# Storing units two by two as 32 KB runs from three output tiles, in a mixture-of-softmaxes kernel bound by its transfers

## The chip, the cores and the metric

One core of one Trainium2 chip. The metric is the device time of one execution in microseconds (us). Executions of the kernel before lie between 780.81 and 781.27 us. All runs told here were of the fast state (none over 1.5% above the fastest of its kernel); where a "slow run" is spoken of in experiment 9, it is the upper of two groups within that state.

## The reference

```python
def reference(logits, prior):            # logits 32x128x4x4096, prior 32x128x4, float32
    prior_probs = softmax(prior)         # over the 4 heads
    softmax = np.exp(logits - logits.max(-1, keepdims=True))
    softmax /= softmax.sum(-1, keepdims=True)          # over the vocabulary of 4096
    return np.sum(prior_probs[..., None] * softmax, axis=2)     # 32x128x4096
```

Cut to what matters: per row, four softmaxes of 4096 numbers are averaged with four weights. 268.5 MB are read and 67.1 MB are written.

## The kernel before

The 4096 rows are cut into 32 units of 128 rows, one row to a partition. Row pairs of a partition lie side by side in memory; a unit takes one row of each pair (`j` is 0 or 1). A unit is loaded into one of two input buffers (64 KB per partition), ACT makes four exponentials with their sums, DVE weights them into an output tile, and ACT's queue stores that tile (16 KB per partition).

```python
ltile = cpool.tile([P, 2, H, V], FP32, name="ltile")      # two input buffers
ebuf1, ebuf3: SBUF tiles; ebuf2: PSUM tile                # exponentials 1, 3, 2
obuf = cpool.tile([P, 2, V], FP32, name="obuf")           # two output tiles

def load(u):        # ... goes out when the unit that held the buffer has been read
    ld = nc.sync.dma_start(out=ltile[:, u % 2, h:to], in_=lg[u // J, u % J, :, h:to, :])
    only(ld, adds[u - 2, 0] if h == 0 else exps[u - 2, to - 1])

def store(u, acc, eng, lo=0, hi=V):
    st = eng.dma_start(out=ov[u // J, u % J, :, lo:hi], in_=acc[:, lo:hi])
    stores[u] = only(st, adds[u, H - 1])
# ... per unit: four exponentials (the store of unit u-1 goes ahead of the fourth),
# then reciprocal, weights, one product (reads the input buffer), three multiply-adds
es = (lt[:, 0], ebuf1, ebuf2, ebuf3)                      # exponential 0 stays in the buffer
```

`only(ins, *keep)` gives an instruction exactly the waits listed. The first DVE operation of a unit, the product of exponential 0, is the last reader of the input buffer, so it releases the load two units on.

The softmax here doesn't subtract the row's maximum and nothing guards it: scores larger than these inputs give would overflow.

## Time and profile before

| | before |
|---|---|
| time | 781.04 us |
| DVE, ACT busy | 67%, 60% of the span |
| DMA queues q1 (loads, last stores), q10 (stores) | 82.3%, 17.6% of sixteen engines |
| a steady unit | 24.2 us |

How to read it: the two queues' packet times are given as shares of sixteen engines' span. Where they add to 100%, no engine of the sixteen has idle time, and waits of ACT or DVE for a load are only the other side of that. The prediction below shows the lines and reads them.

### The profile page before, as it was taken

The numbers are of one execution on the slowest core, as the hardware profiler recorded it, in microseconds if no ns is written. First come the engines' busy times: TensorE is split into PE (matmuls) and PEld (weight loads), VectorE is DVE, ScalarE is ACT, GpSimd is POOL, SyncE is SP. The second block draws the span as 40 slices with busy tenths as digits, with TensorE's granted clock in tenths as the row PEclk, the third lists the DMA queues.
The fourth block names the chain that finished last, engine by engine and source line by source line (L and its number), as shares of the span: only waits on it lengthen the run. The fifth ranks groups of instructions, "written<-read, shape, count | busy, mean of one in ns | idle before, by whom it ended". The sixth has DMA issues, their size and how long they took to land.

```text
span 779.3 us, 654 instructions
## 1 busy us (share of the span) xinstructions
DVE 521.0 (67%) x174; ACT 466.7 (60%) x258; POOL 8.3 (1%) x41
## 2 busy tenths in 40 slices
DVE  4447875558755587555775557855578655689886
ACT  4476555775457755577555675546765567657782
POOL 0000000000000000000000000000000000000000
DMA  9999999999999999999999999999999999999998
GB/s 407 457 417 401 470 407 434 428 461 428 405 467 403 458 420 433 442 443 418 431 454 407 454 408 467 420 415 447 432 442 417 463 399 463 410 427 433 434 429 377
DMA packets 10117, 335.66 MB, mean 431 GB/s; under 512 B 1136, under 2 KB 1136, under 8 KB 1152
## 3 DMA queue, kind: packets, MB, share of 16 engines
q1 hardware_dynamic: 6048, 276.83, 82.3%
q10 hardware_dynamic: 4064, 58.79, 17.6%
q14 instruction: 5, 0.04, 0.0%
HBM read 268.50 MB, written 67.11 MB: 431 GB/s over the span
## 4 chain that ended last, share of the span: by engine, by line
DMA 64%; ACT 27%; DVE 6%; issue 2%; POOL 0%; DVEq 0%; POOLq 0%
DMA ltile<-in_logits_dram 62%; ACT ebuf L159 19%; ACT ltile L159 8%; DVE obuf L177 5%; DMA out_dram<-obuf 2%; DVE ltile L183 1%; POOL coeff L170 0%; DVE rden L168 0%; DVEq L240 0%; POOLq L240 0%; POOLq L170 0%
## 5 line engine op out<-in xcount | busy, mean ns | idle before, releaser
L183 DVE SCALAR_TENSOR_TENSOR obuf<-ebuf,coeff,obuf 128x4096 f32<-128x4096 f32 x90 | 403.6, 4484 | 3.8 <-POOL coeff L170 0.6
L159 ACT ACTIVATE ebuf<-ltile 128x4096 f32<-128x4096 f32 x90 | 322.9, 3589 | 7.4 <-DMA ltile<-in_logits_dram 7.4
L159 ACT ACTIVATE ltile<-ltile 128x4096 f32<-128x4096 f32 x38 | 137.3, 3614 | 280.6 <-DMA ltile<-in_logits_dram 280.6
L168 DVE RECIPROCAL rden<-dsum 128x4 f32<-128x4 f32 (+1 forms) x36 | 6.3, 175 | 227.9 <-ACT ebuf L159 225.1
L177 DVE TENSOR_SCALAR obuf<-ltile,coeff 128x4096 f32<-128x4096 f32 x30 | 70.6, 2353 | 10.2 <-POOL coeff L170 10.2
L183 DVE SCALAR_TENSOR_TENSOR ltile<-ltile,coeff 128x4096 f32<-128x4096 f32 (+1 forms) x7 | 27.0, 3875 | 0.8 <-POOL coeff L170 0.6
L159 ACT ACTIVATION_READ_ACCUMULATOR ebuf<-ltile 128x1 f32 x90 | 16.8, 186 | 0.0
L170 POOL TENSOR_TENSOR coeff<-rden,pp 128x4 f32<-128x4 f32 (+1 forms) x36 | 7.2, 200 | 755.3 <-DVE rden L168 745.4
L159 ACT ACTIVATION_READ_ACCUMULATOR ltile<-ltile 128x1 f32 x38 | 7.1, 186 | 0.0
L139 DVE TENSOR_REDUCE pmax<-pr 16x256 f32<-16x1024 f32 x1 | 1.2, 1208 | 7.8 <-DMA pr<-in_prior_dram 7.8
L141 ACT ACTIVATE pr<-pr 16x1024 f32<-16x1024 f32 x1 | 1.1, 1055 | 7.8 <-DVE pr L140 7.8
L177 DVE TENSOR_SCALAR ltile<-ltile,coeff 128x4096 f32<-128x4096 f32 x2 | 4.7, 2354 | 0.6 <-POOL coeff L170 0.6
L144 DVE TENSOR_TENSOR pn<-pr,pmax 16x1024 f32<-16x1024 f32 x1 | 1.9, 1939 | 0.1
L141 ACT ACT_TABLE_LOAD x1 | 1.3, 1283 | 1.2 <-PEq L229 1.2
L142 DVE TENSOR_REDUCE pmax<-pr 16x256 f32<-16x1024 f32 x1 | 1.2, 1207 | 1.1 <-ACT pr L141 1.1
L149 DVE STREAM_TRANSPOSE pp<-pn 32x256 f32<-32x256 f32 x4 | 1.7, 435 | 0.1
L143 DVE RECIPROCAL pmax<-pmax 16x256 f32<-16x256 f32 x1 | 1.7, 1741 | 0.0
L140 DVE TENSOR_TENSOR pr<-pr,pmax 16x1024 f32<-16x1024 f32 x1 | 1.2, 1211 | 0.0
L138 POOL MEMSET pn<- 32x1024 f32 x1 | 0.9, 941 | 0.3 <-POOLq L229 0.3
L229 POOL MEMSET const-bfloat16-1.0<- 128x1 bf16 x1 | 0.1, 106 | 0.0
L229 POOL MEMSET const-uint8-127<- 128x1 uint8 x1 | 0.1, 106 | 0.0
L229 POOL MEMSET const-float32-0.0<- 128x1 f32 x1 | 0.1, 103 | 0.2 <-issue 0.2
(1 smaller groups left out, 0.1 us busy)
## 6 DMA issues: line engine op xcount, KB each, us to landing
out_dram<-obuf ACTq DMA_DIRECT2D x28, 2048.0 KB, 29.4
ltile<-in_logits_dram SPq DMA_DIRECT2D x7, 4096.0 KB, 26.1
ltile<-in_logits_dram SPq DMA_DIRECT2D x2, 2048.0 KB, 30.9
out_dram<-obuf SPq DMA_DIRECT2D x2, 2048.0 KB, 33.9
out_dram<-ltile SPq DMA_DIRECT2D x1, 2048.0 KB, 17.2
out_dram<-ltile SPq DMA_DIRECT2D x2, 1024.0 KB, 4.8
ltile<-in_logits_dram SPq DMA_DIRECT2D x28, 30.9
pr<-in_prior_dram ACTq DMA_DIRECT2D x1, 64.0 KB, 7.0
```

Of the source, the lines that this page charges most:

```text
L139: nc.vector.reduce_max(pmax, pr, axis=AX.X)
L140: nc.vector.tensor_sub(pr, pr, pmax.unsqueeze(2).to_broadcast([G, R, H]))
L141: nc.scalar.activation(pr, pr, AF.Exp)
L142: nc.vector.reduce_sum(pmax, pr, axis=AX.X)
L143: nc.vector.reciprocal(pmax, pmax)
L144: nc.vector.tensor_mul(pn[0:G].rearrange("g h r -> g r h"), pr, pmax.unsqueeze(2).to_broadcast([G, R, H]))
L149: nc.vector.transpose(pp[32 * t : 32 * (t + 1)], pq[:, :, :, 32 * t : 32 * (t + 1)])
L159: ex = nc.scalar.activation(es[h], lt[:, h], AF.Exp, accum_out=dsum[:, u, h : h + 1])
L168: rc = nc.vector.reciprocal(rden[:, u, h : h + n], dsum[:, u, h : h + n])
L170: mul = nc.gpsimd.tensor_mul(coeff[:, u, h : h + n], rden[:, u, h : h + n], ppu[:, h : h + n])
L177: st = nc.vector.tensor_scalar(out=acc[:, lo:hi], in0=es[h][:, lo:hi], scalar1=coeff[:, u, h : h + 1], scalar2=None, op0=ALU.mult,)
L183: st = nc.vector.scalar_tensor_tensor(out=acc[:, lo:hi], in0=es[h][:, lo:hi], scalar=coeff[:, u, h : h + 1], in1=acc[:, lo:hi], op0=ALU.mu ...
```

## The change

Its intent: the two rows of a partition lie side by side in the output. If two units are stored together, 128 runs of 32 KB replace 256 runs of 16 KB, and half the fixed cost of the store packets goes. It needs a third output tile. There is no room for one more tile, so the tile of the fourth exponential is given up: it goes into an output tile that is free at the time. In even units that is the unit's own tile, and it must then be weighted first, in place.

```diff
+    def row(u):                       # units 2, 3 take row 1 first, so a group's tiles lie in order
+        return u % 2 if u // 2 % 2 == 0 else 1 - u % 2
+    def slot(u):                      # odd units: tile 1; even units: tile 0 and tile 2 in turn
+        return 1 if u % 2 else u // 2 % 2 * 2
+    def store_group(g, eng):
+        lo = g % 2
+        st = eng.dma_start(out=ov[g].rearrange("j p v -> p j v"), in_=obuf[:, lo : lo + 2])
+        stores[2 * g] = stores[2 * g + 1] = only(st, last[2 * g + 1])
-    obuf = cpool.tile([P, 2, V], FP32, name="obuf")
+    obuf = cpool.tile([P, 3, V], FP32, name="obuf")
+                if second:                           # odd unit
+                    es.append((nxt, slot(u + 1)))    # 4th exponential in the next unit's tile
+                    order = (0, 1, 2, 3)
+                else:                                # even unit
+                    es.append((own, slot(u)))        # in its own tile, weighted first
+                    order = (3, 0, 1, 2)
-                if h == H - 1 and 0 < u < U - 3:
-                    store(u - 1, obuf[:, (u - 1) % 2], nc.scalar)
+                if h == 2 and 0 < u < U - 3:         # one exponential earlier than before
+                    if u <= 2 or u > ONE:            # ONE = U - 6
+                        store(u - 1, obuf[:, slot(u - 1)], nc.scalar)
+                    elif not second:
+                        store_group(u // 2 - 1, nc.scalar)
+                if h == H - 1 and second and u < U - 4 and u >= 3:
+                    free[slot(u + 1)] = [stores[u - 3], stores[u - 2]]
```

Cut: the bookkeeping of which operation frees which tile, and the last four units, which use other tiles but do the same work.

More of the change, by code (lines that the diff above doesn't have):

```diff
@@ L92 @@
     stores = {}
+    last = {}
+    ONE = U - 6
+    def row(u):
+        return u % 2 if u // 2 % 2 == 0 else 1 - u % 2
+    def slot(u):
+        return 1 if u % 2 else u // 2 % 2 * 2
     def load(u):
@@ L100, in load @@
             ld = nc.sync.dma_start(
-                out=ltile[:, u % 2, h:to], in_=lg[u // J, u % J, :, h:to, :]
+                out=ltile[:, u % 2, h:to], in_=lg[u // J, row(u), :, h:to, :]
             )
-            if u >= 2:
-                only(ld, adds[u - 2, 0] if h == 0 else exps[u - 2, to - 1])
+            if u < 2:
+                only(ld)
+            elif h == 0:
+                only(ld, adds[u - 2, here(u - 2)])
             else:
-                only(ld)
+                only(ld, exps[u - 2, to - 1])
             for k in range(h, to):
@@ L112, in store, with here @@
     def store(u, acc, eng, lo=0, hi=V):
-        st = eng.dma_start(out=ov[u // J, u % J, :, lo:hi], in_=acc[:, lo:hi])
-        stores[u] = only(st, adds[u, H - 1])
+        st = eng.dma_start(out=ov[u // J, row(u), :, lo:hi], in_=acc[:, lo:hi])
+        stores[u] = only(st, last[u])
+    def store_group(g, eng):
+        lo = g % 2
+        st = eng.dma_start(
+            out=ov[g].rearrange("j p v -> p j v"), in_=obuf[:, lo : lo + 2]
+        )
+        stores[2 * g] = stores[2 * g + 1] = only(st, last[2 * g + 1])
+    def here(u):
+        return 1 if U - 4 <= u < U - 2 else 0
     pr = cpool.tile([G, R, H], FP32, name="pr")
@@ L125 @@
     coeff = cpool.tile([P, U, H], FP32, name="coeff")
-    ebuf1 = cpool.tile([P, V], FP32, name="ebuf1")
-    ebuf2 = psum.tile([P, V], FP32, name="ebuf2")
-    ebuf3 = cpool.tile([P, V], FP32, name="ebuf3")
-    obuf = cpool.tile([P, 2, V], FP32, name="obuf")
+    ebuf = cpool.tile([P, V], FP32, name="ebuf")
+    pbuf = psum.tile([P, V], FP32, name="pbuf")
+    obuf = cpool.tile([P, 3, V], FP32, name="obuf")
     with tc.manual_schedule():
@@ L149, with exp, weigh @@
             nc.vector.transpose(pp[32 * t : 32 * (t + 1)], pq[:, :, :, 32 * t : 32 * (t + 1)])
+        free = {}
         for u in range(U):
-            bufd = u < U - 2
+            second = u % 2
             lt = ltile[:, u % 2]
-            acc = obuf[:, u % 2] if bufd else lt[:, 0]
-            es = (lt[:, 0], ebuf1, ebuf2, ebuf3) if bufd else [lt[:, h] for h in range(H)]
-            ppu = pp[:, u % J, :, u // J]
-            def exp(h, *keep):
-                ex = nc.scalar.activation(
-                    es[h], lt[:, h], AF.Exp, accum_out=dsum[:, u, h : h + 1]
-                )
-                keep = (loads[u, h],) + keep
-                if bufd and h and u:
-                    keep += (adds[u - 1, h],)
-                exps[u, h] = only(ex, *keep)
-            def weigh(h, n, *keep):
+            own = obuf[:, slot(u)]
+            nxt = obuf[:, slot(u + 1)] if second else None
+            if u < U - 4:
+                es = [(lt[:, 0], None), (ebuf, "e"), (pbuf, "p")]
+                if second:
[4 more added lines that the diff above has]
+                    order = (3, 0, 1, 2)
+            elif u == U - 4:
+                es = [(ebuf, "e"), (lt[:, 1], None), (pbuf, "p"), (own, slot(u))]
+                order = (0, 1, 2, 3)
+            elif u == U - 3:
+                own = obuf[:, 2]
+                es = [(own, 2), (lt[:, 1], None), (ebuf, "e"), (pbuf, "p")]
+                order = (0, 1, 2, 3)
+            else:
+                own = lt[:, 0]
+                es = [(lt[:, h], None) for h in range(H)]
+                order = (0, 1, 2, 3)
+            part = ebuf if u == U - 4 else own
+            ppu = pp[:, row(u), :, u // J]
+            def exp(h):
+                t, name = es[h]
+                ex = nc.scalar.activation(t, lt[:, h], AF.Exp, accum_out=dsum[:, u, h : h + 1])
+                exps[u, h] = only(ex, loads[u, h], *free.get(name, []))
+            def weigh(hs):
+                h, n = min(hs), len(hs)
                 rc = nc.vector.reciprocal(rden[:, u, h : h + n], dsum[:, u, h : h + n])
-                only(rc, exps[u, h + n - 1])
+                only(rc, *[exps[u, k] for k in hs])
                 mul = nc.gpsimd.tensor_mul(
@@ L172, in weigh, with add @@
                 )
-                return only(mul, rc, *keep)
-            def add(h, mul, lo=0, hi=V):
-                if h == 0:
+                return only(mul, rc)
+            def add(k, mul, lo=0, hi=V):
+                h = order[k]
+                t, name = es[h]
+                c = coeff[:, u, h : h + 1]
+                if k == 0:
                     st = nc.vector.tensor_scalar(
-                        out=acc[:, lo:hi], in0=es[h][:, lo:hi], scalar1=coeff[:, u, h : h + 1],
-                        scalar2=None, op0=ALU.mult,
+                        out=part[:, lo:hi], in0=t[:, lo:hi], scalar1=c, scalar2=None,
+                        op0=ALU.mult,
@@ L180, in add @@
                     )
-                    adds[u, h] = only(st, mul)
+                    only(st, mul)
                 else:
                     st = nc.vector.scalar_tensor_tensor(
-                        out=acc[:, lo:hi], in0=es[h][:, lo:hi], scalar=coeff[:, u, h : h + 1],
-                        in1=acc[:, lo:hi], op0=ALU.mult, op1=ALU.add,
-                    )
-                    adds[u, h] = only(st, mul, adds[u, h - 1])
-            free = (stores[u - 2],) if bufd and u >= 2 else ()
+                        out=(own if k == H - 1 else part)[:, lo:hi], in0=t[:, lo:hi],
+                        scalar=c, in1=part[:, lo:hi], op0=ALU.mult, op1=ALU.add,
+                    )
@@ L191 @@
+                    only(st, mul, last[u])
+                adds[u, h] = last[u] = st
+                if name is not None:
+                    free[name] = [st]
             m = H if u < U - 4 else 2
             for h in range(H):
-                late = h == H - 1 and 4 <= u < U - 3
-                if h == H - 1 and 0 < u < U - 3:
-                    store(u - 1, obuf[:, (u - 1) % 2], nc.scalar)
-                exp(h, *((stores[u - 4],) if late else ()))
+                if h == 2 and 0 < u < U - 3:
[3 more added lines that the diff above has]
+                        store_group(u // 2 - 1, nc.scalar)
@@ L197 @@
+                if h == H - 1 and second and u < U - 4 and u >= 3:
+                    free[slot(u + 1)] = [stores[u - 3], stores[u - 2]]
+                if u == U - 3 and h == 0:
+                    free[2] = [stores[u - 3]]
+                exp(h)
                 if (h + 1) % m:
                     continue
-                g = h + 1 - m
-                mul = weigh(g, m, *(free if g == 0 else ()))
-                for k in range(g, h + 1):
+                mul = weigh(range(h + 1 - m, h + 1))
@@ L202 @@
+                for k in range(h + 1 - m, h + 1):
                     n = 2 if u == U - 1 and k == H - 1 else 1
@@ L206 @@
                         if n > 1:
-                            store(u, acc, nc.sync, c * w, (c + 1) * w)
+                            store(u, own, nc.sync, c * w, (c + 1) * w)
+            if u == U - 4:
+                free["e"] = [last[u]]
             if u + 2 < U:
@@ L210 @@
             if u == U - 3:
-                store(u - 1, obuf[:, (u - 1) % 2], nc.sync)
-                store(u, acc, nc.sync)
+                store(u - 1, obuf[:, slot(u - 1)], nc.sync)
+                store(u, own, nc.sync)
             elif u == U - 2:
-                store(u, acc, nc.sync)
+                store(u, own, nc.sync)
 _INS = ['logits', 'prior']
```

## The prediction

> **What bounds the kernel now.** I read the page of before from the top. The slices and the DMA queues come first, because no compute engine is over 67% busy (DVE 67%, ACT 60%).
>
> ```profile
> DMA  9999999999999999999999999999999999999998
> ...
> DMA packets 10117, 335.66 MB, mean 431 GB/s; under 512 B 1136, under 2 KB 1136, under 8 KB 1152
> ...
> q1 hardware_dynamic: 6048, 276.83, 82.3%
> q10 hardware_dynamic: 4064, 58.79, 17.6%
> ```
>
> All 40 slices of the DMA row are at 90% or more but the last, and the two queues' packets take 82.3 + 17.6 = 99.9% of sixteen engines' span. q1 is the sync engine's queue (the loads and the last stores), q10 is ACT's (28 stores). So the sixteen DMA engines have no idle time to give back. The chain that ended last and the waits agree: the chain is 64% DMA, ACT waits for loads, and the load queue waits for the first DVE operation on a unit, which frees the input buffer.
>
> ```profile
> DMA 64%; ACT 27%; DVE 6%; issue 2%; POOL 0%; DVEq 0%; POOLq 0%
> ...
> ACT ltile L159 <- DMA ltile<-in_logits_dram: 280.6, 32, 12.0
> ...
> SPq L100 <- DVE obuf L177: 702.8, 30, 31.0
> ```
>
> The ACT and DVE parts of that chain are not time that could be saved: while it runs through them, the engines carry the other unit's load and a store. The timeline of one steady unit shows by how much the loads are ahead:
>
> ```profile
> 379.04 3.62 ACT L159 ACTIVATE ltile<-ltile 128x4096 f32<-128x4096 f32 x1 [9.67 <-DMA ltile<-in_logits_dram]
> ...
> 385.83 0.34 ACTq L113 DMA_DIRECT2D out_dram<-obuf  x1
> ...
> 394.07 2.35 DVE L177 TENSOR_SCALAR obuf<-ltile,coeff 128x4096 f32<-128x4096 f32 x1 [0.32 <-POOL coeff L170]
> 396.45 72.85 SPq L100 DMA_DIRECT2D ltile<-in_logits_dram  x4
> 396.46 13.53 DVE L183 SCALAR_TENSOR_TENSOR obuf<-ebuf,coeff,obuf 128x4096 f32<-128x4096 f32 x3
> 403.21 3.62 ACT L159 ACTIVATE ltile<-ltile 128x4096 f32<-128x4096 f32 x1 [9.67 <-DMA ltile<-in_logits_dram]
> ```
>
> A unit lands at 379.0 and the next at 403.2, so a unit takes 24.2 us. The load two units on is issued at 396.45, 17.4 us after the landing: 6.8 us before the load ahead of it has ended. The queue never runs dry, and that margin is what the change can lose. Sixteen such units, seen through the DMA view and the windows view, give the price of a packet:
>
> ```profile
> q1 hardware_dynamic: 2303, 134.15, 80.0%
> q10 hardware_dynamic: 2304, 33.56, 20.2%
> ...
> 258.14:645.07 386.93, 255.75 (x81) 232.09 (x128) 3.21 (x16) 1.00 1.00 433
> ```
>
> q10 moved 33.56 MB, which is 2048 packets of 16 KB (and 256 of semaphores), in 0.202 x 16 x 386.93 us = 1251 us: 611 ns each. q1 moved about 2047 packets of 64 KB in 0.800 x 16 x 386.93 = 4953 us: 2.42 us each. The packet records of the whole trace, by size, have medians of 611 ns for 16 KB, 1213 ns for 32 KB and 2418 ns for 64 KB. That is a straight line: 602 ns per 16 KB and 9 ns per packet. The shares add to 100.2%, so neighbouring packets overlap: 0.002 x 16 x 386.93 us over 4095 data packets is 3 ns each. About 6 ns of the 9 ns then really cost time. Start to start, eight 32 KB packets of one engine near the end (738.96 to 748.64, one semaphore packet of 9 ns in it) make 1209 ns each, and eight of 16 KB (748.64 to 753.50) 606 ns. There a merge saves 2 x 606 - 1209 = 3 ns. So I take 3 to 9 ns, 6 in the middle.
>
> **What the Trainium skill says.** Its page "DMA: Bandwidth & Descriptors" bears on this in four places. Where 436 GB/s comes from: 16 ports of 32 B at 850 MHz, 435.2 GB/s. The trace agrees: 433 GB/s in the steady part, so only half a per cent is left there. Why small descriptors are slow: a fixed cost of about 3 cycles per packet. At 850 MHz that is 3.5 ns, an estimate from the page, and the bottom of my 3 to 9 ns. Queues, rings and completion order: each DMA engine takes turns between the queues for which it has work. The packet records show a 64 KB load and a 16 KB store in turn on an engine (381.29, 383.70, 384.31, 386.73 us). Specifications: an HBM limit of some 358 GB/s per core. The trace has 431 GB/s over the span with this core alone, so the measurement decides and that limit doesn't bind here.
>
> **The change part by part.**
>
> Removed: units 2 to 25 are 24 units of 128 rows. 3072 store packets of 16 KB become 1536 of 32 KB, because the two rows of a partition lie side by side in the output and in the output tiles. 1536 x 6 ns / 16 engines = 0.58 us (0.3 at 3 ns, 0.9 at 9 ns). Twelve DMAs fewer save one 9 ns semaphore packet per engine each, 12 x 9 ns = 0.1 us. Sum: 0.7 us, all of it on the path, because the DMA engines are the path.
>
> Added: nothing on ACT (128 exponentials of 3.6 us) or DVE (32 products of 2.35 us, 96 multiply-adds of 4.48 us, one of them in two halves). The order of the instructions in the changed kernel, compared engine by engine, has the same kinds and counts. Bytes are the same. In-place products cost the same: at the end of before they take 2354 ns.
>
> Moved: three things, all into the 6.8 us of margin.
> - In even units the exponential that sits in the output tile is weighted first. The operation that reads the input buffer is then second, so the load two units on goes out 4.5 us later.
> - ACT now issues the store ahead of its third exponential rather than its fourth, and that store waits for the last DVE operation of the unit before. The third exponential can be held up.
> - The fourth exponential of odd units waits for the store of the group before, now 4 MB in one piece.
>
> Is there still always a packet to move? Call s the moment when a group's store is issued, which is the moment when DVE ends the odd unit. The odd buffer's next load went out 13.5 us before (three multiply-adds). The even buffer's next load follows the store by two exponentials (7.6 us with the start), 0.5 us to the product, 2.4 us and 4.5 us: 15.0 us. Between those loads lie 28.5 us. The work queued for each engine meanwhile is 8 x 2.41 us of load (381.29 to 383.70 us above) and 8 x 1.209 us of store, 29.0 us, even if both queues were empty at the start. So in the worst case the bus is covered with 0.5 us to spare, and at the pace of before with more. The engines finish a transfer up to 0.9 us apart (semaphore packets at 401.84 and 402.76 us), so a single engine can idle for a few tenths of a us. In the other half the even load brings 19.3 us of its own. A full pair has 16 loads and 8 stores per engine, 48.3 us, and both chains between two stores (through the odd load, and through the store and the fourth exponential) can close in less when the queues thin. DMA stays the bound. The thinnest place is unit 4, just after the single stores: its load goes out near 88 us instead of 82.0, when load 3 drains at 87.5 and only some four 16 KB packets (2.4 us) of store 1 are left. I allow 0.2 us for it on average.
>
> The end is built as before: the last five stores go behind the loads on the sync queue, and the same halves close it. Total: 781.04 - 0.7 + 0.2 = 780.5 us.
>
> **Rivals.**
>
> 1. **The bus goes idle.** For it: the margin shrinks from 6.8 us to 0.5 us in the worst case, and the first store of before came to its first packet only 4.4 us after its issue (46.17 to 50.61 us). If 2 us were lost in each of the 12 groups, the time would be 780.3 + 24 = 804 us, 3% slower; once, near unit 4, 782 us. Against it: a late load loses nothing while store packets are there, since the other queue takes the engine, and issue delay shifts both queues alike. Beside idle engines a load's first packet came 1.0 us after its issue.
> 2. **The store becomes a ring of waits.** Store, fourth exponential, weighting, four DVE operations, next store: in strict turns 8 x (1.209 + 2.41) = 29.0 us of store, up to 4.4 us of start, 3.6 + 0.5 + 15.9 us of compute: 53 us over 48.3 us, which would be 12 x 5 = 60 us, 840 us. Against it: strict turns need a load in the queue all the time. When loads run out, eight stores need 9.7 us alone and the ring closes in about 34 us. It can only move bytes from one queue to the other.
> 3. **Longer runs gain nothing**, or the writes gain more than the packet count says. The first gives 781.0 us. The second has a floor: 335.66 MB at 435.2 GB/s is 771.3 us, against 777 us from the first load packet (1.0 us) to the last store packet (778.0 us). Even removing every loss would give 775 us, under 1%.
>
> **Range and chances.** The gain lies between 0.4 and 1.0 us and an idle gap costs 0 to 1.5 us, which gives 779.8 to 781.6 us. Over 2% faster is below the floor of rival 3. Over 2% slower needs rival 1 or 2 in every group: 2%.
>
> **What would show it.** Right: q10 with 12 x 16 = 192 + 1536 fewer packets (4064 to 2336), the DMA row still at 9 throughout, the queues' shares still adding to 99.9%, the load queue waiting for a multiply-add in even units, landing intervals of loads uneven (short without a store beside them, long with one) but 48.3 us per pair. Wrong: slices of the DMA row below 9, long waits of ACT for a store, a pair of units over 48.5 us, or packets of 32 KB that write in another time than 1213 ns.

## The result, and the profile after

| | before | after |
|---|---|---|
| median | 781.02 us (780.84 to 781.11, 6 runs) | 783.3 us (782.94 to 784.95, 6 runs) |
| ratio | | 1.0032, 95% interval 1.0019 to 1.0045 |
| span in the profile | 779.3 us | 781.2 us |

The change made the kernel 2.3 us slower, within 2% but outside the predicted range. Ratios here are the mean time of one kernel's runs over that of the other's of the same rounds, so they are not quite the ratio of the medians quoted.

From the page of after: the DMA slices, the packets, the queues (packets, MB, share of sixteen engines), and the shares of the chain that ended last.

```profile
DMA  9999999999999999999999999999999999999998
...
DMA packets 8388, 335.65 MB, mean 430 GB/s; under 512 B 944, under 2 KB 944, under 8 KB 960
...
q1 hardware_dynamic: 6048, 276.83, 82.4%
q10 hardware_dynamic: 2336, 58.79, 17.5%
...
DVE 41%; DMA 33%; ACT 22%; issue 3%; POOL 1%; ACTq 0%; SPq 0%; POOLq 0%
```

The packet count is as predicted: q10 has 2336 packets for 4064. The DMA row has no slice under 9 but the last, and the queues add to 99.9%. By these rows the engines still have no idle time, and yet the same bytes took 1.9 us longer. The chain now is 41% DVE and 33% DMA. Such a chain changes its looks when two waits nearly tie, and does not tell by itself that DVE is the bound.

The waits of after (engine, line, waited for, us in total, times, longest), and those of the sync queue that issues the loads:

```profile
ACT ltile L208 <- DMA ltile<-in_logits_dram: 243.8, 31, 12.1
...
ACT pbuf L208 <- DVE obuf L231: 17.9, 22, 2.7
...
ACT obuf L208 <- DMA out_dram<-obuf: 3.7, 4, 1.1
```

```profile
SPq L112 <- DVE obuf L231: 418.9, 15, 35.5
SPq L112 <- DVE obuf L225: 271.4, 14, 21.7
```

ACT waited 17.9 us for DVE ahead of its third exponential: that is the store issue, which stands before it in ACT's stream and waits for the odd unit's last multiply-add. It waited only 3.7 us for stores. Fifteen of the 29 loads now wait for a multiply-add (L231), the second operation of an even unit, as predicted. What this does to the first such load is seen in the timeline of before, then of after (start, duration, engine, line; in brackets the idle time before). The first line of each is the issue of the load of unit 4, the second the first exponential on the load ahead of it:

```profile
82.00 0.33 SPq L100 DMA_DIRECT2D ltile<-in_logits_dram  x1
...
88.15 3.62 ACT L159 ACTIVATE ltile<-ltile 128x4096 f32<-128x4096 f32 x1 [9.06 <-DMA ltile<-in_logits_dram]
```

```profile
87.84 0.33 SPq L112 DMA_DIRECT2D ltile<-in_logits_dram  x1
...
88.04 3.62 ACT L208 ACTIVATE ltile<-ltile 128x4096 f32<-128x4096 f32 x1 [7.63 <-DMA ltile<-in_logits_dram]
```

Before, the load is issued 6.1 us before the one ahead of it has landed. After, 0.2 us before. The load of unit 6 is issued 0.7 us after the one ahead has landed, and in the even units from 8 on the margin is 1.0 to 2.0 us for 6.8 us.

**Where the time went.** I kept a ledger from the packet records of each trace: the time since the start, less the bytes moved so far at 435.2 GB/s, the rate of the sixteen ports that the Trainium skill gives ("DMA: Bandwidth & Descriptors", Where 436 GB/s comes from; the steady 433 GB/s agree). It grows by what the packets cost beyond their bytes, and by what is lost.

```
ledger, us     at 88    130    250    400    650    700    770
before          3.0    3.2    3.7    4.2    5.1    5.3    5.8
after           2.9    4.6    5.2    5.8    6.8    7.3    7.7
```

Of 1.9 us, 1.5 are lost between 88 and 130 us (after loses 1.62 us there, before 0.14), 0.3 near the end of the groups (650 to 700), and some 0.2 to 0.3 in between, most of it before 250 us (at 88 us after was 0.1 ahead). It shows in the packets, not as idle time: the 3584 packets of 64 KB have a mean of 2420.9 ns before and 2431.6 ns after, 10.7 x 3584 / 16 = 2.4 us. Of that, 1.4 us sit in packets in flight at 89.7 us (up to 1318 ns too long), when the late load of unit 4 starts, and at 121 to 128 us (up to 1203 ns, on all engines), when the first group store starts. Most of the rest is spread over the steady part, where the mean is 2422.6 ns for 2418.1.

In the steady part the change neither wins nor loses. Sixteen units of before, and sixteen of after, by the windows view (stretch, its length, busy time of DVE, ACT and POOL, clock, DMA share, GB/s):

```profile
282.32:669.23 386.91, 255.74 (x81) 232.09 (x128) 3.21 (x16) 1.00 1.00 433
```

```profile
281.56:668.56 387.00, 256.61 (x81) 233.88 (x128) 3.24 (x16) 1.00 1.00 433
```

386.91 and 387.00 us. The saving of eight groups should have been 8/12 of 0.7 us, 0.5 us.

### The profile page after: what moved, and what is told of

It reads as the page before. It is cut to its first block, busy times and chain, and to the rows that moved or that the text cites. A ratio compares the mean times of both kernels' runs of the same rounds, so it can differ in the third digit from the quotient of the medians.

```text
span 781.2 us, 617 instructions
## 1 busy us (share of the span) xinstructions
DVE 521.1 (67%) x174; ACT 470.1 (60%) x258; POOL 8.4 (1%) x41
## 3 DMA queue, kind: packets, MB, share of 16 engines
q10 hardware_dynamic: 2336, 58.79, 17.5%
## 4 chain that ended last, share of the span: by engine, by line
DVE 41%; DMA 33%; ACT 22%; issue 3%; POOL 1%; ACTq 0%; SPq 0%; POOLq 0%
DVE obuf L231 31%; DMA ltile<-in_logits_dram 22%; DMA out_dram<-obuf 11%; ACT obuf L208 9%; ACT pbuf L208 8%; DVE obuf L225 6%; ACT ltile L208 3%; ACT ebuf L208 2%; DVE ltile L231 1%; DVE ebuf L231 1%; POOL coeff L215 1%; DVE rden L213 1%; ACTq L132 0%; DVE ebuf L225 0%; ACTq L127 0%
## 5 line engine op out<-in xcount | busy, mean ns | idle before, releaser
L231 DVE SCALAR_TENSOR_TENSOR obuf<-ebuf,coeff,obuf 128x4096 f32<-128x4096 f32 x29 | 130.1, 4484 | 1.3 <-POOL coeff L215 0.3
L231 DVE SCALAR_TENSOR_TENSOR obuf<-pbuf,coeff,obuf 128x4096 f32<-128x4096 f32 x29 | 130.0, 4484 | 1.0
L208 ACT ACTIVATE pbuf<-ltile 128x4096 f32<-128x4096 f32 x30 | 107.5, 3584 | 20.9 <-DVE obuf L231 17.9
L208 ACT ACTIVATE ebuf<-ltile 128x4096 f32<-128x4096 f32 x30 | 108.1, 3602 | 18.1 <-DMA ltile<-in_logits_dram 16.0
L208 ACT ACTIVATE obuf<-ltile 128x4096 f32<-128x4096 f32 x30 | 108.0, 3601 | 3.7 <-DMA out_dram<-obuf 3.7
L231 DVE SCALAR_TENSOR_TENSOR obuf<-ltile,coeff,obuf 128x4096 f32<-128x4096 f32 x15 | 67.3, 4484 | 0.5
L231 DVE SCALAR_TENSOR_TENSOR obuf<-obuf,coeff 128x4096 f32<-128x4096 f32 x14 | 62.8, 4485 | 0.5
L225 DVE TENSOR_SCALAR obuf<-obuf,coeff 128x4096 f32<-128x4096 f32 x15 | 35.3, 2353 | 4.7 <-POOL coeff L215 4.7
L225 DVE TENSOR_SCALAR obuf<-ltile,coeff 128x4096 f32<-128x4096 f32 x14 | 32.9, 2353 | 4.4 <-POOL coeff L215 4.4
L231 DVE SCALAR_TENSOR_TENSOR ltile<-ltile,coeff 128x4096 f32<-128x4096 f32 (+1 forms) x7 | 27.1, 3876 | 0.8 <-POOL coeff L215 0.6
L208 ACT ACTIVATION_READ_ACCUMULATOR ebuf<-ltile 128x1 f32 x30 | 5.6, 186 | 0.0
L231 DVE SCALAR_TENSOR_TENSOR ebuf<-pbuf,coeff,ebuf 128x4096 f32<-128x4096 f32 x1 | 4.5, 4484 | 0.3 <-POOL coeff L215 0.3
L231 DVE SCALAR_TENSOR_TENSOR ebuf<-ltile,coeff,ebuf 128x4096 f32<-128x4096 f32 x1 | 4.5, 4485 | 0.0
```

Source lines behind the costliest of these rows:

```text
L208: ex = nc.scalar.activation(t, lt[:, h], AF.Exp, accum_out=dsum[:, u, h : h + 1])
L225: st = nc.vector.tensor_scalar(out=part[:, lo:hi], in0=t[:, lo:hi], scalar1=c, scalar2=None, op0=ALU.mult,)
L231: st = nc.vector.scalar_tensor_tensor(out=(own if k == H - 1 else part)[:, lo:hi], in0=t[:, lo:hi], scalar=c, in1=part[:, lo:hi], op0=ALU. ...
```

## The experiments

Each table of times has the median, the range, the number of runs, and the ratio to the kernel before in the same rounds with its interval. "Margin" is the landing of a load less the issue of the next one.

### 1. The change once more

No edit.

> The changed kernel, not edited, for a second profile and more times. Its first profile loses 1.9 us on the 781.0 us of before: packets of 64 KB that were in flight when a store queue or a load queue that had been empty started again took up to 1.3 us longer than 2418 ns (2.4 us over sixteen engines, 1.1 of it at the first group store near 124 us, 0.4 near 90 us). Theory 'queue restarts': 782.9 to 784, and a second profile again shows 64 KB packets whose mean is over 2425 ns, with the loss near 90 and 124 us. Rival 'chance': the two stalls of the first profile are accidents; then they lie elsewhere and times scatter from 780.5 upward.

783.39 us (782.83 to 783.69, 5 runs), 1.0031 (1.0018 to 1.0045). The mean packet of 64 KB is 2430.5 ns, the stalls are again at 89.8 us (0.3 us over sixteen engines) and from 121.5 us (1.1 us), and sixteen units take 386.95 us. The loss is no accident.

### 2. Two stores of 16 KB packets in place of the group's one

```diff
-        st = eng.dma_start(out=ov[g].rearrange("j p v -> p j v"), in_=obuf[:, lo : lo + 2])
+        for j in range(J):
+            st = eng.dma_start(out=ov[g, j], in_=obuf[:, lo + j])
```

> The changed kernel, but each group is stored by two DMAs of 2 MB with 16 KB packets, issued together where the one of 32 KB packets was. Everything else (order, waits, three output tiles) is as in the change. Theory 'schedule and restarts': the loss stays, and the packets cost 0.5 us more again: 783.5 to 784.5. Rival '32 KB store packets disturb': the loss goes with them, 780.8 to 781.5.

793.57 us (793.3 to 798.02, 5 runs), 1.0173 (1.0153 to 1.0192). Neither number was expected: ten us slower than the change. So the 32 KB packets are not what disturbs; in this schedule they help. Packets of the two queues go in turns, so the share of a store depends on its packet size.

### 3 and 4. All stores in the loads' queue

```diff
-                        store_group(u // 2 - 1, nc.scalar)
+                        store_group(u // 2 - 1, nc.sync)
```

The single stores likewise; and in the second kernel the stores of before.

> The changed kernel with all its stores issued from the sync engine's queue instead of ACT's, so that loads and stores go one after the other in one queue that is never empty, and no store issue sits between ACT's exponentials. Theory 'queue restarts': the loss goes, the saving of fewer packets shows: 780.0 to 780.9. Rival 'shorter margin leaves engines idle': loads go out as late as in the change, so the loss stays, 782.5 or more. Rival 'a queue in strict order makes stores wait behind a load': a store lands later and the fourth exponential waits: over 784.

> The kernel before with its 28 ACT stores issued from the sync engine's queue. 16 KB packets in one queue. Theory: before has hardly any restart loss, so 780.6 to 781.3, and against the other one-queue kernel it gives the price of 1536 packets without two queues: 0.3 to 0.9 us longer.

783.75 us (783.13 to 784.41, 5 runs), 1.0035 (1.0022 to 1.0048), for the change in one queue, and 783.71 us (783.67 to 784.32, 5 runs), 1.0037 (1.0024 to 1.005), for before in one queue. The theory misses in both. 783.75 lies in the range of the rival 'shorter margin', but the kernel before, whose loads wait for the same instruction as ever, loses as much, 2.7 us, in one queue. So one queue is no cure. 32 KB runs show no gain over 16 KB runs there either, 783.75 against 783.71, though these two kernels differ in their schedules too. My wording "queue restarts" was too simple.

### 5. The change's schedule with single stores

```diff
-    ONE = U - 6
+    ONE = 0
```

> The changed kernel with no groups: every unit is stored alone (28 ACT stores of 2 MB in 16 KB packets), but the three output tiles, the row order, the order of operations in even units and the earlier place of the store in ACT's stream stay. Theory A 'stores in bursts': the time is lost where a store starts after a stretch with loads alone, so without groups the store queue stays filled and the time is that of before, 780.8 to 781.5. Theory B 'the order and the later loads cost': the loss stays, 782.5 or more.

790.13 us (789.87 to 796.73, 6 runs), 1.0142 (1.0112 to 1.0171). Packets and bytes are those of before, so the 9 us come from the schedule alone: the reading "only bursts cost" fell. In the trace the even loads have a margin of 2.4 us. They start late, the store then runs without a load beside it and lands after 22 us instead of 29, the store queue is empty for some 2.6 us, and where the next store starts, load packets on all engines take 0.2 to 0.9 us longer, some 0.5 us in the sum over sixteen engines, once in every pair.

### 6 and 7. Groups in one half of the run only

```diff
-                    if u <= 2 or u > ONE:                 # late groups: 7 to 12
+                    if u <= 14 or u > ONE:
-    ONE = U - 6                                           # early groups: 1 to 6
+    ONE = 14
```

> Groups for units 14 to 25 only (6 groups of 32 KB packets), single stores before. In both profiles of the full change the ledger (time minus bytes moved at the fabric's rate) loses 1.1 us at the first group store and some 0.3 us at the load of unit 4, and little in the later groups. If that belongs to the first group store after a stretch of loads alone, wherever it comes, it is found again at the store of group 7 near 410 us and the time is 781.8 to 782.5. If it belongs to the first 130 us of the run, it is gone: 780.6 to 781.2.

> Groups for units 2 to 13 only, single stores after. The early part is that of the full change, so both readings expect its early loss: 782.2 to 783. The rest, with single stores, should run as before does; a time as long as that of the full change (783.3) would say that later groups cost nothing net, one near 782.5 that they cost the difference.

789.62 us (788.77 to 790.44, 4 runs), 1.011 (1.0097 to 1.0124), and 787.02 us (786.41 to 788.77, 4 runs), 1.0081 (1.0067 to 1.0095). Both are longer than expected, because the parts with single stores lose as the kernel of experiment 5 does (3.5 us in 200 us with early groups, where before loses 0.7). One thing can be read: with late groups the change-over from single stores to groups has its loss too, 0.6 us near 405 us and 0.7 us from 418.8 us. So that loss belongs to the change-over, not to the first 130 us of a run.

### 8 and 9. The store issued ahead of the fourth exponential

```diff
-                if h == 2 and 0 < u < U - 3:
+                if h == H - 1 and 0 < u < U - 3:
```

> The full change, with the store issued ahead of the fourth exponential as before has it, not the third, so that the third is not held up (ACT waited 17.9 us for DVE there) and the even loads go out 1 to 3 us earlier. Theory A: the stretches without stores are the same, so 782.8 to 783.6. Theory B: part of the loss goes, under 782.3.

784.34 us (781.67 to 787.03, 6 runs), 1.0043 (1.0017 to 1.0069). The runs fall in two groups: 781.67, 781.9, 782.04 and 786.64, 786.73, 787.03. The profile is of the first. Its steady part is the cleanest test of the price of packets, with hardly a slow packet in it. Sixteen units by the windows view, and the queues in that stretch (packets, MB, share):

```profile
250.87:637.83 386.96, 255.75 (x80) 232.97 (x128) 3.21 (x16) 1.00 1.00 434
```

```profile
q1 hardware_dynamic: 2304, 134.22, 80.1%
q10 hardware_dynamic: 1152, 33.55, 20.1%
```

1152 packets on q10 for 2304, and 386.96 us for the 386.93 that the prediction quotes of before. **Merging saved nothing.** By the ledger, a pair of units of before has 32 packets on each engine at 5.5 ns beyond their bytes (semaphores included), 176 ns. Here it has 24 at 7.2 ns, 173 ns. The lengths in the packet records tell why. A packet overlaps with the one after it on its engine by some 4 ns, the same in both kernels and whether a load or a store comes next. From start to start, the median packet of 64, 32 and 16 KB takes 2414, 1209 and 607 ns, some 4.6 ns more than its bytes at 435.2 GB/s, and a semaphore packet 6 ns. So eight groups should have saved 0.34 us. But the packets that stayed became longer. In these units of before every load packet but one takes 2418 ns (mean 2418.1). Here the mean is 2419.9, and that of the 32 KB stores 1214.2 for 1213: together 0.3 us. Where loads follow one another without stores, from 23 to 39 us of before, the mean is 2421.6 ns. A load packet was shorter where it took turns with stores, and with half the store packets there are fewer turns; why that is so, the records do not say.

The same trace shows late loads that cost nothing (load issue, first exponential on the load ahead):

```profile
326.67 0.33 SPq L112 DMA_DIRECT2D ltile<-in_logits_dram  x1
...
328.90 3.62 ACT L208 ACTIVATE ltile<-ltile 128x4096 f32<-128x4096 f32 x1 [9.66 <-DMA ltile<-in_logits_dram]
```

The margin is 2.2 us in every even unit from 8 to 26, no load packet moves for 3.0 to 3.2 us of each pair, and the store queue is empty for some 20 us before each store is issued. Yet from 190 to 660 us one load packet is 0.4 us too long (512.8 us), and no other by more than 0.1 us.

I ran the same kernel again for the slow group.

> The full change with the later store issue once more: its runs fell in two groups, 781.7 to 782.0 and 786.6 to 787.0. In the profile of the fast group store and ring of waits made 48.35 us per pair, just what the bytes need. Expected: two groups again, and if the profile is of the slow one, pairs of over 48.5 us from some point on, with ACT waiting for stores.

786.32 us (781.8 to 788.67, 4 runs), 1.0048 (1.0027 to 1.007): both groups again, and the profile is of a slow run (788.67 us). ACT's wait for stores, in the profile of the fast run and then in that of the slow run:

```profile
ACT obuf L208 <- DMA out_dram<-obuf: 15.4, 12, 2.1
```

```profile
ACT obuf L208 <- DMA out_dram<-obuf: 29.9, 12, 7.2
```

Twelve waits of up to 2.1 us became twelve of up to 7.2 us. In the fast run a store takes 28.1 us and the way from its landing to the next issue 20.2 us, 48.3 us per pair, exactly what the bytes need. In the slow run the first stores take 29.9, 29.7 and 32.6 us, store follows store after 50.1, 49.9 and 52.8 us, the odd loads go out late (margins of 3.0, 3.0 and 0.6 us for units 7, 9 and 11, where the fast run has 5.5 to 6.4), that of unit 12 has a margin of 0.1 us, and by 350 us the ledger stands 6.6 us over that of the fast run. This is the ring of waits of the prediction's second rival, on the edge of binding.

### 10 and 11. Late loads in the kernel before

```diff
-                only(ld, adds[u - 2, 0] if h == 0 else exps[u - 2, to - 1])
+                only(ld, adds[u - 2, 1 if 2 <= u - 2 < U - 6 else 0] if h == 0 else exps[u - 2, to - 1])
```

The second kernel has `and u % 4 == 0` in the condition.

> The kernel before, with one wait moved: the loads for units 4 to 27 go out after the second DVE operation of the unit that held the buffer, not the first, 4.5 us later (6.8 us of margin become 2.3). Stores, packets, tiles and order are those of before. Theory 'a late load costs even while stores are queued': the load queue runs dry, the stores go alone and end early, the store queue runs dry too, and each start of a store beside loads costs 0.4 to 0.8 us, as in the kernel with single stores: 24 units make 786 to 795. The prediction's own view 'the other queue takes the engine, nothing is lost': 780.9 to 781.5.

> The same, but only every fourth load is late (units 4, 8 to 24: six of them). If each late load costs by itself, a quarter of what the kernel with all loads late loses, 782 to 784; if one late load is made up by the margin of the next three, 780.9 to 781.5.

788.85 us (788.23 to 790.7, 4 runs), 1.0105 (1.0092 to 1.0118), and 784.31 us (784.14 to 786.2, 5 runs), 1.0049 (1.0037 to 1.0061). One wait was moved; tiles, order, packets and stores are those of before. 24 late loads cost 7.9 us, 0.33 us each; six cost 3.3 us, 0.56 us each, a little over the range given for them. A late load is not made up by the next three. A unit of the first kernel in the timeline (load issue, first exponential on the load ahead, store issue):

```profile
281.60 0.33 SPq L100 DMA_DIRECT2D ltile<-in_logits_dram  x1
...
284.20 3.62 ACT L159 ACTIVATE ltile<-ltile 128x4096 f32<-128x4096 f32 x1 [10.03 <-DMA ltile<-in_logits_dram]
...
290.65 0.34 ACTq L113 DMA_DIRECT2D out_dram<-obuf  x1
```

The load goes out 2.6 us before the one ahead has landed (6.8 us in before). On one engine of this trace the last load packet ends at 281.37 us, six 16 KB store packets follow back to back, and the next load packet starts at 285.03 us: 3.4 us after the issue. The engine was never idle, but the store queue was used up and stayed empty until the store of 290.65. The load packets in flight when that store starts (295.7 us) take up to 314 ns longer. DMA shows 9 in every slice but the last here too.

### 12. Weak point of experiment 5: single stores, issued later

```diff
-    ONE = U - 6
+    ONE = 0
-                if h == 2 and 0 < u < U - 3:
+                if h == H - 1 and 0 < u < U - 3:
```

> The change's three tiles and order, all stores single, and the store ahead of the fourth exponential as before has it. The even loads go out about 1.5 to 3 us earlier than in the kernel with single stores ahead of the third (margin 2.4 us there). Theory: the margin becomes 4 to 5 us, and most of the 9 us lost there come back: 781 to 785. If the lateness of the loads isn't the cause: 789 to 791.

792.52 us (789.93 to 795.09, 5 runs), 1.0159 (1.0146 to 1.0172). A miss of mine, and a failed test: the even loads still have margins of 2.2 to 2.7 us, since the loads ahead of them land earlier too. The dose was not changed, so the run says nothing on the lateness.

### 13. Store starts without late loads

```diff
-            cuts = (0, H)
+            cuts = (0, 2, H)
-                keep = (loads[u, h],) + keep
+                keep = ((loads[u, h],) if u == 0 or u >= U - 3 else (loads[u, 0], loads[u, 2])) + keep
```

> The kernel before, with each load of units 1 to 28 as two DMAs of 2 MB (32 KB packets); the exponentials still wait for both, so compute and the issue of the loads keep their places. In turns with 32 KB packets a 16 KB store has twice the share: 8 x 1.82 = 14.5 us instead of 24, so the store queue is empty for a third of every unit and each store starts anew beside loads, while the load queue keeps its margin of some 6.8 us. If a store's start costs 0.4 to 0.8 us by itself: 28 starts, 790 or more. If a start is harmless while the load queue has its margin, and only the dry load queue costs: 781 to 782.

783.64 us (783.51 to 783.86, 5 runs), 1.0034 (1.0022 to 1.0046). The median store from issue to landing, in before and here:

```profile
out_dram<-obuf ACTq DMA_DIRECT2D x28, 2048.0 KB, 29.4
```

```profile
out_dram<-obuf ACTq DMA_DIRECT2D x28, 2048.0 KB, 18.5
```

The store ends in 18.5 us, and the store queue is empty for about 6 us of every unit, while the load margin stays at 6.8 us. After the first store (48 us) no store start has slow load packets. So a start is harmless by itself. That it isn't the 32 KB load packets that make it harmless is seen in experiment 16. The time lies over the 781 to 782 of that reading mainly because of the packets: from 250 to 550 us the ledger grows by 1.84 us for 1.10, with 99 more packets on each engine, 7.5 ns each, and up to 770 us it makes 1.7 of the 2.6 us. The other 0.9 come after 770 us, in the last stores, and I did not follow them up. Packets added to the loads do cost what packets were predicted to cost; packets taken from the stores gave nothing back on balance.

### 14 and 15. Weighting two and two, then with 32 KB load packets

The change, with reciprocal, weight and product of the first two operations done while ACT is at the later exponentials; even units make the exponentials in the order 0, 1, 3, 2. The core:

```diff
-                mul = weigh(range(h + 1 - m, h + 1))
+                ks = {2: (0, 1), 3: (2, 3)} if order[0] == 3 else {1: (0, 1), 3: (2, 3)}
+                muls = {k: weigh([order[k]]) for k in ks.get(n_, ())}
-                only(ld, adds[u - 2, here(u - 2)])
+                only(ld, adds[u - 2, here(u - 2)], *early(u - 2))    # and the last exponential
-                    only(st, mul)
+                    only(st, mul, *([stores[u - 2]] if second and 3 <= u < U - 4 else []))
```

The second kernel also has loads in two halves, as in experiment 13.

> The full change with 32 KB groups, but the exponentials weighted two and two: in even units in the order 0, 1, 3, 2, so that the products of 3 and 0 are done while ACT works on the last one, and the loads go out 3 to 4 us earlier than in the change (18.3 us after the landing in even units, 14.5 to 16.5 in odd ones). Theory: the loss near units 4 and 5 and at the group starts goes, and as 32 KB packets save nothing in steady state (sixteen units took 386.96 us with them and 386.93 without), the time is that of before: 780.7 to 781.5. With the saving of the prediction it would be 780.3. If 32 KB groups cost by themselves: 783 or more.

> The kernel with two-and-two weighting, with loads in 32 KB packets too. Theory 'ring of waits': there, store (33 us from issue to landing) and the odd unit's four DVE operations with the way to the next issue (16.5 us) made 49.3 us per pair, more than the 48.4 us of the bytes. Stores in turns with 32 KB packets need some 20 to 25 us, so the ring is down to 37 to 42 us and the kernel is bound by bytes again: 780.3 to 781.5. If the ring is not the cause: 785 or more as before.

786.97 us (783.74 to 788.89, 6 runs), 1.0071 (1.0054 to 1.0088), and 784.98 us (784.83 to 785.06, 5 runs), 1.005 (1.0038 to 1.0062). Both are outside what I expected. In the first, the load margins are 5.7 to 8.2 us from unit 4 up to 490 us, and from 90 to 450 us the ledger grows by 1.12 us where that of before grows by 1.34: with a full load queue the groups do save 0.2 us in some seven pairs, 0.03 us a pair. Then it falls behind. Its waits for stores, and the median of its twelve group stores from issue to landing:

```profile
DVE obuf L228 <- DMA out_dram<-obuf: 86.4, 12, 10.7
ACT obuf L211 <- DMA out_dram<-obuf: 45.6, 9, 7.2
```

```profile
out_dram<-obuf ACTq DMA_DIRECT2D x12, 4096.0 KB, 32.8
```

The store takes 32.8 us, because a load is always there to take turns with it. From its landing through the odd unit's product and three multiply-adds to the next issue there are 16.5 us. Together 49.3 us, for 48.4 us of bytes. The margin shrinks pair by pair, to 3.5 us after 540 us, and from 507 us on packets are slow at the starts. With 32 KB load packets the same store takes:

```profile
out_dram<-obuf ACTq DMA_DIRECT2D x12, 4096.0 KB, 23.9
```

Store follows store after 48.4 to 49 us then, so the ring no longer binds, and the scatter of the times went from 5 us to 0.2 us. That the ring was the cause in the first kernel fits this, but it is read from the traces: the new load packets change more than the ring. 1.3 us remain over experiment 13, where the load packets are the same. They are lost after 450 us, most of them in slow packets at 505 to 509 us (0.6 us) and 567 to 576 us (0.4 us).

### 16. The change with 32 KB load packets

Edit as in experiment 13.

> The changed kernel with loads in 32 KB packets, nothing else. The loads still go out as late, and the stores end sooner, so the load queue runs dry with no store left to fill in: theory 'late loads' 784 to 800, more than the change (783.3). If only the share of the stores matters: 781 or less.

790.57 us (786.37 to 792.77, 6 runs), 1.0114 (1.009 to 1.0138). The theory of late loads expected this: shorter stores leave less to fill in with. The loss is 7.3 us greater than in the change, of which 2.6 us are what the 32 KB load packets cost before too (experiment 13). Load packets are up to 1.9 us too long here, though they are of 32 KB, and an engine was idle for 1.2 us on average.

### 17. The late load of unit 4 taken away

```diff
+                elif u <= 2:                              # units 0 and 2: the tile still free
+                    es.append((obuf[:, 2 - u], 2 - u))
+                    order = (0, 1, 2, 3)
```

The waits for that tile's store and last reader were added.

> The full change, but in units 0 and 2 the fourth exponential goes to the output tile that is still free there (tile 2, tile 0), so these two units keep the order 0, 1, 2, 3 of before and the loads for units 2 and 4 go out 4.5 us and some 4 us earlier (unit 4's near 83.5 us instead of 87.84). From unit 4 on all is as in the change. In the ledger the change loses 1.45 us against before between 88 and 130 us and nothing in steady state. If the late load of unit 4 starts that loss, it goes, and the time is 781.5 to 782.1. If the first group store loses 1.1 us by itself, 782.6 or more.

783.37 us (782.99 to 784.42, 5 runs), 1.0034 (1.002 to 1.0048). The time missed both expectations; the trace tells them apart all the same. The load of unit 4 now has a margin of 4.6 us, no packet near 90 us is slow, and the first group store costs 0.2 us instead of 1.1. The first group store by itself is not the cause. But the load of unit 6 is now 2.3 us late (after the landing, not before it), and the next starts cost 0.5 us (169.6 us) and 0.4 us (266.7 us). The ledger ends 1.6 us over before, instead of 1.9. The loss moved on with the late load. But lateness alone does not set its size: in the change itself the load of unit 6 came 0.7 us after the landing, and the next store's start cost 0.1 us.

## Why the prediction was wrong

**The saving.** The step "1536 x 6 ns / 16 engines = 0.58 us", with 0.1 us for semaphores, was mis-sized: on balance it measured 0.0 us (387.00 and 386.95 us for sixteen units of the change in its two profiles, 386.96 in experiment 8, 386.91 and 386.93 before), and at most 0.03 us a pair, 0.4 us in all, where the loads were early (experiment 14). The straight line through the packet durations was right, and the records confirm it: 32 KB stores take 1213 ns. The price of a packet was a little too high: 4.6 ns from start to start, not 6. (The prediction's own stretch from 738.96 to 753.50 us gives 4.9 and not 3, since the semaphore packet in it takes 6 ns from start to start and not 9.) That leaves 0.5 of the 0.7 us. What failed is the assumption that the other packets keep their length. They took the rest back: load packets of 2419.9 ns in experiment 8 and of 2422.6 ns in the change, for 2418.1.

**The late loads.** The step that failed is in rival 1: "a late load loses nothing while store packets are there, since the other queue takes the engine". Experiment 10 moved only the loads of before by 4.5 us, and lost 7.9 us with no engine idle. Experiment 13 showed the starts of stores harmless with loads in time. So late loads can cost time although stores keep the engines busy, where they go out and at the next store's start. They don't always: no load packet moves for 3.2 to 5.5 us in every pair of the change from unit 6 on, and for some 3 us in the fast run of experiment 8, and sixteen units take 387.00 and 386.96 us. In the change the slow packets were fewest where many packets of the group store were left when the loads came back (none left at unit 4, 1.4 us; 12 to 20 left, 0.03 us or less), but in experiment 10 the loads of units 4 to 6 found at most one left and lost 0.02 us. When a late load costs is not shown. I had the thinnest place right, unit 4, and its load at 87.84 us for "near 88"; I allowed 0.2 us for it, and 88 to 130 us cost 1.5 us.

**The engines stay covered.** This was right as said (the queues add to 99.9%, the DMA row is at 9, and by the packet records an engine was idle for 0.04 us on average between 6 and 770 us) and misled me: a row of 9s does not say that packets move at their best rate.

**The ring of waits.** Right for the change itself, where ACT waited 3.7 us for stores. But "It can only move bytes from one queue to the other" was wrong in general: with loads early, the ring was 49.3 us per pair and, by its trace, bound (experiment 14), and in the slow runs of experiment 9 it fell behind. My reading of these runs, not a thing shown, is that the change lies between two limits: loads late enough to keep the stores short, and early enough that the load queue isn't dry for long.

**The moved parts** were right: the even load a multiply-add later, ACT's third exponential held up, nothing added on DVE.

The chances were right in kind: the change stayed within 2%.

What stays open: why load packets take longer when some stores start after the load queue has run dry, and not at others, and why they are 2 to 4 ns shorter in turns with stores. The records give a packet's start, length and queue, and not which memory it waits for. Nothing that I ran beats the kernel before.

## What to carry to other kernels

When the transfer queues are full, fewer and longer packets may bring nothing: measure the price of a packet in the place where it will be saved, next to the same neighbours. Count how long before its predecessor lands a load is issued, and keep that margin unless a run shows that it isn't needed. A full DMA row doesn't show that time is lost in the packets; the mean length of equal packets does.

## What the Trainium skill lacked or had wrong

- "DMA: Bandwidth & Descriptors", Why small descriptors are slow: a fixed cost of about 3 cycles per packet. The page does not say that a packet's time depends on what runs beside it. The runs show, beyond the bytes and from start to start, 4.6 ns per packet where loads and stores take turns, 8.5 ns where 64 KB loads follow one another (before, 23 to 39 us), and nothing saved on balance by 1536 fewer store packets.
- The same page, Queues, rings and completion order: turns by packet are described, with some 9 to 17 descriptors in one. Here a turn is one run of 16 to 64 KB, and it is not said that run lengths therefore set each queue's share: a 2 MB store took 29.4 us beside 64 KB loads and 18.5 us beside 32 KB loads.
- No page: that loads issued late can cost time although stores keep the engines busy, 7.9 us for 24 loads issued 4.5 us later in the kernel before, and can also cost nothing (386.96 us for sixteen units in experiment 8).
- The same page, Specifications and Where 436 GB/s comes from: an HBM limit of some 358 GB/s per core, said to bind for transfers between HBM and SBUF, in those sections without the condition that both cores of a pair are active, which the page gives only beside its measured figures. This core, alone, moved 433 GB/s. "Perfetto Trace Analysis", Roofline has it right: a core that is alone is bounded by its 16 DMA engines, at about 435 GB/s.
